# Cached keys turned beside the even layer and kept turned in a scratch area

## The chip, the cores and the metric

The kernel runs on one core of a Trainium2 chip. The metric is the device time of one execution in microseconds (us); lower is better. Engines are named as in the profile: PE (TensorE, the matrix engine), PEld (its weight loads), DVE (VectorE), ACT (ScalarE), POOL (GpSimd) and SP (SyncE, whose queue issues nearly all DMAs).

## The reference

One inference step of a two-layer decoder, for a prompt of 2048 tokens and for 8 sequences of 4 new tokens each ("the sample", 32 tokens), model width 1024. Layer 0 (even) has HGRN2 heads (a gated linear recurrence) beside four heads of forgetting attention; layer 1 (odd) is a gated linear attention (GLA). The part that matters here is the sample's attention over a paged cache: each of 8 sequences owns 16 pages of 128 tokens, 4 heads, 128 values a head, in float32.

```python
k_past = k_pages[page_table].reshape(db, -1, H, dh)
v_past = v_pages[page_table].reshape(db, -1, H, dh)
...
logit_past = jnp.einsum('bthd,bshd->bhts', q, k_past).astype(jnp.float32) * scale \
    + cum_new[..., None] + suffix_past[:, :, None, :]
...
p = jax.nn.softmax(jnp.concatenate([logit_past, logit_new], axis=-1), axis=-1).astype(v.dtype)
return jnp.einsum('bhts,bshd->bthd', p[..., :P], v_past) + jnp.einsum('bhts,bshd->bthd', p[..., P:], v)
```

That is 8 x 16 = 128 pages of keys and as many of values, 256 KB each.

## The kernel before

The kernel has three phases.

**Even layer** (`phase_even`). The prompt is worked in two halves of 1024 tokens (the sample goes with the first). Each half has 16 projection units (`order`), a unit being 256 or so columns of the input weights times all tokens of the half; `staged` (L1261) runs a unit's matmuls and puts, between their steps, the fetch, measuring, scaling and splitting of the weights of the units two and three ahead. In the first half the weights come as float32 into tiles of tag `wr` (three buffers), are split into two float16 parts (tag `w`) and stored to the scratch `wd`; in the second half they are loaded from `wd`, and `wr` isn't used. The recurrences (`lin`) run between units. `staged` also calls `beside(x)` twice a unit, at its second and fourth step, with x = 2j and 2j + 1 for the unit j of 32. For x from 33 on, `beside` fetches and measures the weights of the 20 units of the later projections: `later_unit` (L386) loads them into four tiles of tag `lr` (eight buffers) and takes four reductions (L303) of them.

**Attention** (`phase_fox`). `fox_prompt` runs 16 groups (4 heads by 4 query blocks of 512); a group loads q, k, bias, v and gate (L1375 to L1390) on SP's queue, forms scores (PE L626 to L628), adds bias and takes the maximum (DVE, L1413), exponentiates, turns the weights by PE (L1449), splits them (ACT L1456, DVE L1457) and multiplies them with the values. `fox_sample` is interleaved with it by costs: `until` takes from the one or the other by the sum of the costs that each yields. It first works through the cached keys, then through the cached values:

- Keys: 32 tiles, each of one page of four sequences. `pages` loads four page numbers into SP's registers (L1533) and issues four DMAs (L1546) into a tile of tag `pg` (six buffers, shared with the pages of values), 32 partitions a page. `turn` transposes the tile by four DVE instructions in blocks of 32 x 32 (L1590) into a tile of tag `kt` (two buffers), so that the head's dimension lies on the partitions. One tile later `strips` issues 16 matmuls, four heads side by side on strips of the array (L1647; the profile has two records for each). The transposes are held behind a few evictions of the prompt (`KAHEAD`), and the requests of pages behind the eighth request before them (`asked[-8]`).
- Values: 34 steps of pages in the same way, 128 partitions a page, used as they land (L1723).

**Odd layer** (`phase_odd`): output projection of layer 0, then layer 1 and the outputs.

The order of instructions on each engine is made when the kernel is built, by a planner that models their times; `issue_after` puts an instruction behind another one in it. Each engine and SP's queue then work strictly in that order. A tile waits until the tile that had its memory before is free, also across the pools of two phases: the attention's tiles on the right side lie where the even layer's weights and activations were.

Of the kernel before, what the change touches and what calls it, by code (L numbers as in the profile page):

```python
# [8 lines left out]
F32 = mybir.dt.float32  # L9
# [10 lines left out]
P = 128  # L20
# [8 lines left out]
NH = 4  # L29
EPS = 1e-6  # L30
WU = 272
# [3 lines left out]
SC_C = 1350.0  # L35
# [4 lines left out]
EWR = 3  # L40
# [7 lines left out]
REST_P = 18000.0  # L48
REST_S = 12200.0
PG = 6  # L50
PAST = 3
VAHEAD = 3
KAHEAD = 6
# [2 lines left out]
WSPLIT = 4  # L56
# [55 lines left out]
def drain(g):  # L112
    for _ in g:
        pass
# [11 lines left out]
class Kern:  # L126
# [6 lines left out]
    def consts(self):  # L133
        nc, i = self.nc, self.i
        cp = self.ctx.enter_context(self.tc.tile_pool(name="const", bufs=1))
        self.cp = cp

        def col(name, ap, n):
            t = cp.tile([P, n], F32, name=name)
            with nc.allow_non_contiguous_dma(reason="small constant vectors"):  # L140
                nc.sync.dma_start(t, ap.rearrange("(k p) -> p k", p=P))
            return t

        self.ident = cp.tile([P, P], F32, name="ident")
# [241 lines left out]
    def later_unit(self, pool, pps, w, cols, key, undo=None):  # L386

        nc = self.nc
        h, width, t = KT // WSPLIT, sum(n for _, n in cols), {}

        def fetch():
            t["raw"] = [pool.tile([P, h, WU], F32, tag="lr", name=f"lr_{key}{a}") for a in range(WSPLIT)]
            for a, off, n, src in self.sources(w, cols, h):
                with nc.allow_non_contiguous_dma(reason="a few columns"):
                    nc.sync.dma_start(t["raw"][a][:, :, off : off + n], src)

        def parts():
            t["m"] = pool.tile([P, WSPLIT + 1], F32, tag="rm", name=f"rm_{key}")
            return [r[:, :, :width] for r in t["raw"]]

        return (fetch,) + self.unit_scale(key, parts, lambda: t["m"], pool, pps, key, undo, 1.0)

# [716 lines left out]
    def phase_even(self):  # L1119
        tc, nc, i = self.tc, self.nc, self.i  # L1120
        def pool(name, **kw):
            return tc.tile_pool(name=name, bufs=1, reuse_waits="tile", **kw)

        with pool("act", side="right") as ap, pool("w", side="right") as w0, pool("wl", side="right") as wp1, \
                pool("wk") as wp0, pool("nrm") as n0, pool("stt") as sp, pool("ps", space=PSUM) as pp0:
            wpool = Pool(w0, {"w": 3, "wr": EWR, "rm": 2, "pow": 2, "lr": 8})
            wp = Pool(wp0, {"c4": 7, "sam": 1, "v4": 3, "sg": 3, "pd": 1, "kt": 2, "y": EY, "xpad": 1, "vs": 3,
                            "ss": 2, "rs_t": 2, "rs_r": 2}, Pool(wp1, {"c2": EC2, "th": ETH}))
            pps = Pool(pp0, {"pj": 3, "gr": 2, "st": 1, "o": 2})
# [26 lines left out]
            for hf in range(2):  # L1156
# [64 lines left out]
                if hf == 0:  # L1221
# [13 lines left out]
                    ahead = [g[0] for g in nxt[:3]]  # L1235
                else:
                    ahead = []
# [264 lines left out]
    def strips(self, makers, sources):  # L1502
# [8 lines left out]
                last = m()  # L1511
        return last

    def fox_sample(self, fs, pps):


        nc, i = self.nc, self.i
        fc = fs
        n_pool = i["cache_fox_k"].shape[1]

        def one(shape, name, dt=F32):
            return fs.tile(shape, dt, tag=name, name=name)

        regs, asked = [None] * 4, []

        def pages(cache, g, j):

            vals = self.tab[:, 4 * g : 4 * g + 4, j]
            with ExitStack() as st:

                if len(asked) >= 8:
                    st.enter_context(self.tc.issue_after(asked[-8].ins))
                _, regs[:] = nc.values_load_multi_w_load_instructions(  # L1533
                    vals, (mybir.EngineType.SP,), min_val=0, max_val=n_pool - 1)
            t = fs.tile([P, 4, 512], F32, tag="pg", name=f"pg{cache}{g}{j}")
            r = []
            for x in range(4):
                src = i[cache][0, bass.ds(regs[x], 1)]
                if cache == "cache_fox_k":
                    dst, src = t[32 * x : 32 * x + 32], src.rearrange("o (k s) h d -> s (o k) (h d)", s=32)  # L1540
                else:
                    dst, src = t[:, x], src.rearrange("o s h d -> (o s) (h d)")
                with ExitStack() as st:
                    if len(asked) < 8:
                        st.enter_context(self.tc.issue_after(first_v.ins))
                    r.append(nc.sync.dma_start(dst, src))  # L1546
# [37 lines left out]
        def turn(t, g, j):  # L1584

            kt = fs.tile([P, NH * 4, P], F32, tag="kt", name=f"kts{g}{j}")
            for x in range(4):
                steps.append(self.last_l)
                with self.tc.issue_after(steps[max(0, len(steps) - KAHEAD)].ins):
                    ins.append(nc.vector.transpose(kt[:, :, 32 * x : 32 * x + 32],  # L1590
                                                   t[:, x].rearrange("p (a e) -> p a e", e=32)))
                yield SC_C
            kts.append(kt)

        env = {}

# [146 lines left out]
        m = self.spread(ys.rearrange("p h b t -> p (h b t)"), pps, "kt", "ys")  # L1743
# [491 lines left out]
```

## Time and profile before

| | |
|---|---|
| median of 3 runs | 2324.5 us (2317.44 to 2325.11) |
| the profiled execution | 2326.98 us |
| its span | 2325.3 us |
| granted clock of PE, mean | 0.981 |
| DMA traffic | 361.93 MB, mean 156 GB/s |

In the profile a row of a stretch gives, for each engine, the busy time and the number of instructions in it; "PEclk" is the clock granted to PE as a share of full speed, "DMA share" the mean share of the core's 16 DMA engines whose packets were under way (it can pass 1). A row of a group gives line, engine, operation, written tile <- read tiles, shapes and count, then busy time and mean ns, then the idle time of the engine before these instructions and what ended most of it. A row of waits reads: engine and line that waited <- what it waited for: us in total, times, the longest.

### The profile page before, as it was taken

To read this page: it belongs to the slowest core of one execution; us is meant where nothing else is said; L and a number is where in the kernel's file an instruction comes from. 1 tells how busy PE (TensorE), PEld (TensorE's weight loads), DVE (VectorE), ACT (ScalarE), POOL (GpSimd) and SP (SyncE) were. 2 spreads that over 40 slices of the span, in tenths; PEclk is the share of its full clock that TensorE was granted. 3 is DMA by queue.
4 is the path that set the end of the run, shared out by engine and by line. 5 is a ranking of instruction groups with operands and counts; after the bars stand their busy time and mean duration, and the time that the engine had idled before them with its cause. 6 is when DMAs were issued, how large, how long until landed. Compare 5 with 4: busy or idle time off the path is not lost.

```text
span 2325.3 us, 58045 instructions
## 1 busy us (share of the span) xinstructions
PE 2211.1 (95%) x23316; PEld 1578.4 (68%) x23316; DVE 1403.4 (60%) x3138; ACT 992.3 (43%) x2200; POOL 727.7 (31%) x788
## 2 busy tenths in 40 slices
PE   7999999999999997788999999999999999999998
PEld 5677677865755874455446888677677666667887
DVE  7756558525644657897668445366665655547554
ACT  6434344211212223355567443555544644545343
POOL 2223424001201223223346245144451432322232
PEclk9999999999999997899999999999999999999999
DMA  7343444755431379999884969424224431115553
GB/s 238 120 126 102 145 133 153 208 146 157 145 120 66 126 185 234 211 225 266 269 268 154 310 200 260 123 75 146 76 92 94 126 92 58 49 56 164 161 196 150
DMA packets 359536, 361.93 MB, mean 156 GB/s; under 512 B 107889, under 2 KB 302770, under 8 KB 355170
## 3 DMA queue, kind: packets, MB, share of 16 engines
q1 hardware_dynamic: 357122, 351.59, 52.3%
q0 software_dynamic: 2144, 6.62, 0.8%
q8 instruction: 183, 3.00, 0.6%
q14 instruction: 87, 0.71, 0.1%
HBM read 244.80 MB, written 96.42 MB: 147 GB/s over the span
## 4 chain that ended last, share of the span: by engine, by line
PE 60%; DMA 8%; DVE 6%; issue 2%; SPq 2%; ACT 2%; POOL 2%; DVEq 0%; POOLq 0%; ACTq 0%
PE pt_o L626 4%; PE pt_o L627 4%; PE pt_o L628 4%; DMA pgcache_fox_k<-in_cache_fox_k 3%; PE pt_Cv L626 2%; PE pt_Cv L628 2%; PE pt_Cv L627 2%; PE pt L1449 1%; PE pv L1723 1%; PE o_C L910 1%; PE gl_C L757 1%; DMA fsg<-sgd 1%; PE pt_Bv L626 1%; PE pt_Bv L628 1%; PE pt_Bk L628 1%
## 5 line engine op out<-in xcount | busy, mean ns | idle before, releaser
L626 PE MATMUL pt_o<-w_o,act 128*128 128x256 f16 x1024 | 279.0, 273 | 1.4 <-ACT sg1C L683 1.2
L627 PE MATMUL pt_o<-w_o,act 128*128 128x256 f16 x1024 | 279.0, 273 | 0.0
L628 PE MATMUL pt_o<-w_o,act 128*128 128x256 f16 x1024 | 278.8, 273 | 0.0
L626 PEld LDWEIGHTS <-act 128*128 128x128 f16 x2304 | 226.0, 98 | 37.9 <-issue 3.5
L627 PEld LDWEIGHTS <-act 128*128 128x128 f16 x2304 | 226.1, 98 | 31.3 <-issue 2.9
L628 PEld LDWEIGHTS <-act 128*128 128x128 f16 x2304 | 226.0, 98 | 29.9 <-issue 2.0
L790 POOL TENSOR_TENSOR kA<-kA,fA 128x512 f32<-128x512 f32 (+1 forms) x56 | 77.1, 1377 | 340.4 <-PE gl_A L757 275.6
L1421 ACT ACTIVATE L<-L,nm,kc 128x512 f32<-128x512 f32 (+3 forms) x160 | 118.2, 741 | 71.7 <-DVE nm L1419 70.5
L628 PE MATMUL pt_Cv<-w_Cv,act 128*128 128x256 f16 (+1 forms) x512 | 141.4, 276 | 0.0
L626 PE MATMUL pt_Cv<-w_Cv,act 128*128 128x256 f16 (+1 forms) x512 | 141.4, 276 | 0.0
L627 PE MATMUL pt_Cv<-w_Cv,act 128*128 128x256 f16 (+1 forms) x512 | 141.4, 276 | 0.0
L1429 POOL TENSOR_SCALAR L<-L,nm 128x512 f32<-128x512 f32 (+3 forms) x160 | 99.8, 638 | 130.7 <-DVE nm L1425 58.9
L1456 ACT ACTIVATE th<-pt 128x512 f16<-128x512 f32 (+3 forms) x159 | 81.9, 528 | 125.6 <-PE pt L1449 124.7
L790 POOL TENSOR_TENSOR kC<-kC,fC 128x512 f32<-128x512 f32 (+1 forms) x56 | 80.5, 1437 | 138.6 <-PE gl_C L757 92.4
L1449 PE MATMUL pt<-ident,L 128*128 128x128 f32 x544 | 93.6, 288 | 12.7 <-DVE tl L1457 11.7
L1590 DVE STREAM_TRANSPOSE kts<-pgcache_fox_k 128x512 f32<-128x512 f32 x128 | 84.4, 693 | 29.9 <-DMA pgcache_fox_k<-in_cache_fox_k 28.4
L1457 DVE TENSOR_TENSOR tl<-pt,th 128x512 f16<-128x512 f32 (+3 forms) x159 | 93.8, 603 | 13.1 <-ACT th L1456 11.9
L1449 PEld LDWEIGHTS pt<-ident,L 128*128 128x128 f32 x544 | 67.8, 147 | 42.3 <-DVE tl L1457 18.7
L626 PE MATMUL s<-k,q 128*128 128x512 f16 (+3 forms) x160 | 58.4, 366 | 31.5 <-DVE mx L1413 31.2
L789 DVE TENSOR_TENSOR qC<-qC,fC 128x512 f32<-128x512 f32 (+1 forms) x56 | 72.9, 1302 | 21.1 <-PE gl_C L757 21.1
L1923 ACT ACTIVATE vC<-pt_Cv,kc 128x512 f32<-128x512 f32 (+1 forms) x40 | 23.9, 599 | 133.1 <-PE pt_Cv L628 133.0
L789 DVE TENSOR_TENSOR qA<-qA,fA 128x512 f32<-128x512 f32 (+1 forms) x56 | 70.0, 1251 | 12.5 <-PE gl_A L757 12.4
(958 smaller groups left out, 6469.5 us busy)
## 6 DMA issues: line engine op xcount, KB each, us to landing
pgcache_fox_k<-in_cache_fox_k SPq DMA_DIRECT2D x128, 256.0 KB, 9.4
pgcache_fox_v<-in_cache_fox_v SPq DMA_DIRECT2D x128, 256.0 KB, 4.5
yr<-yT SPq DMA_DIRECT2D x16, 1024.0 KB, 7.2
x1d<-xo SPq DMA_DIRECT2D x44, 256.0 KB, 4.7
wr_o<-in_w_out_even SPq DMA_DIRECT2D x32, 256.0 KB, 5.3
xo<-in_x_prompt SPq DMA_DIRECT2D x32, 256.0 KB, 5.1
wr_Cv<-in_w_in_odd SPq DMA_DIRECT2D x32, 256.0 KB, 3.6
x1r<-x1d SPq DMA_DIRECT2D x16, 512.0 KB, 4.4
```

The lines of the kernel that those rows point to most:

```text
L626: nc.tensor.matmul(ps, lh[0], rh[0], start=first, stop=False)
L627: nc.tensor.matmul(ps, lh[0], rh[1], start=False, stop=False)
L628: return nc.tensor.matmul(ps, lh[1], rh[0], start=False, stop=last)
L789: nc.vector.tensor_tensor(xv[:, :, 1], xv[:, :, 1], t0.to_broadcast([P, nb, w]), ALU.mult)
L790: nc.gpsimd.tensor_tensor(kv[:, :, 0], kv[:, :, 0], t1.to_broadcast([P, nb, w]), ALU.mult)
L1421: self.last_exp = nc.scalar.activation(lt[:, :w], lt[:, :w], AF.Exp, bias=nm[:, 0:1], scale=ib, accum_out=nm[:, 2 + j : 3 + j])
L1429: nc.gpsimd.tensor_scalar(lt[:, :w], lt[:, :w], nm[:, 1:2], 2.0**14, ALU.mult, ALU.mult)
L1449: nc.tensor.transpose(pt[:, w : w + P], rows[b][s // 4][0][:, (s % 4) * P : (s % 4 + 1) * P], self.ident)
L1456: nc.scalar.activation(th[:, a:w], pt[:, a:w], AF.Copy),
L1457: nc.vector.tensor_tensor(tl[:, a:w], pt[:, a:w], th[:, a:w], ALU.subtract)))
L1590: ins.append(nc.vector.transpose(kt[:, :, 32 * x : 32 * x + 32], t[:, x].rearrange("p (a e) -> p a e", e=32)))
L1923: r = nc.scalar.activation(v[h][:, g : g + cnt], ps[:, :, :256], AF.Copy, scale=c)
```

## The change

Tiles 0 to 27 of the cached keys (`PRE` = 28 of 32) are loaded and transposed in the even layer, stored to a new scratch area `kT` in DRAM, and fetched from it in the attention. The other four go the old way.

- `ahead(pool, y)` is called by each `beside`, with x less 8 (`PRE0`), so from the fifth unit on. At an even step it stores the tile turned in the step before, takes a raw tile, loads the next four page numbers and issues the four page DMAs. At the odd step it takes a second tile and has four DVE transposes turn the raw one into it. Both tiles have tag `lr` while x < 32 (first half) and `wr` from then on. The last store is made after the even layer's last unit.
- `later_unit` takes one tile of four parts instead of four tiles; tag `lr` has two buffers of four times the size.
- In the attention `turned(n)` takes a `pg` tile and fills it by one DMA of 1 MB, 8 KB a partition. It has no register load, is put behind nothing but (for the first two) the prompt's first values load, and is read by the strip matmuls where it landed; the tag `kt` isn't used for it. `strips` waits for that DMA instead of for four transposes. The cost yielded for a tile is the same sum in one piece.

```diff
+PRE = 28
+PRE0 = 8
...
+        self.kT = dp.tile([PRE, P, 4 * 512], F32, name="kT")
...
-            t["raw"] = [pool.tile([P, h, WU], F32, tag="lr", name=f"lr_{key}{a}") for a in range(WSPLIT)]
+            t["raw"] = pool.tile([P, WSPLIT, h, WU], F32, tag="lr", name=f"lr_{key}")
...
-                    nc.sync.dma_start(t["raw"][a][:, :, off : off + n], src)
+                    nc.sync.dma_start(t["raw"][:, a, :, off : off + n], src)
...
-            wpool = Pool(w0, {"w": 3, "wr": EWR, "rm": 2, "pow": 2, "lr": 8})
+            wpool = Pool(w0, {"w": 3, "wr": EWR, "rm": 2, "pow": 2, "lr": 2})
...
             def beside(x):
+                self.ahead(wpool, x)
                 x -= 33
...
             drain(last)
+            self.ahead(wpool, 64)
...
+    def turn_block(self, kt, t, x):
+        return self.nc.vector.transpose(kt[:, :, 32 * x : 32 * x + 32], t[:, x].rearrange("p (a e) -> p a e", e=32))
+
+    def ahead(self, pool, y):
+        y -= PRE0
+        if y % 2:
+            if y // 2 < PRE and y > 0:
+                t, tag = self.key
+                self.key = pool.tile([P, NH * 4, P], F32, tag=tag, name=f"kT{y // 2}"), y // 2
+                for x in range(4):
+                    self.turn_block(self.key[0], t, x)
+            return
+        n = y // 2
+        if 0 < n <= PRE:
+            kt, m = self.key
+            self.nc.sync.dma_start(self.kT[m], kt.rearrange("p a s -> p (a s)"))
+        if 0 <= n < PRE:
+            tag = "lr" if y + PRE0 < 32 else "wr"
+            t = pool.tile([P, 4, 512], F32, tag=tag, name=f"kp{n}")
+            with ExitStack() as st:
+                if n:
+                    st.enter_context(self.tc.issue_after(self.last_page.ins))
+                regs = self.page_regs(n % 2, n // 2)
+            for x in range(4):
+                self.last_page = self.page_load(t, "cache_fox_k", regs[x], x)
+            self.key = t, tag
...
+        def turned(n):
+            kt = fs.tile([P, NH * 4, P], F32, tag="pg", name=f"ktd{n}")
+            with ExitStack() as st:
+                if len(asked) < 8:
+                    st.enter_context(self.tc.issue_after(first_v.ins))
+                d = nc.sync.dma_start(kt.rearrange("p a s -> p (a s)"), self.kT[n])
+            asked.extend([d] * 4)
+            kts.append((kt, [d]))
...
-                yield from turn(pages("cache_fox_k", g, j)[0], g, j)
+                if n < PRE:
+                    turned(n)
+                    yield 4 * SC_C
+                else:
+                    yield from turn(pages("cache_fox_k", g, j)[0], g, j)
...
-            kt = kts.pop(0)
+            kt, made = kts.pop(0)
             self.pks.append(self.strips([score(h, g, j, x, kt, sc) for x in range(4) for h in range(NH)],
-                                        ins[4 * n - 4 : 4 * n]))
+                                        made))
```

More of the change, by code (lines that the diff above doesn't have):

```diff
@@ L391, in fetch @@
         def fetch():
-            t["raw"] = [pool.tile([P, h, WU], F32, tag="lr", name=f"lr_{key}{a}") for a in range(WSPLIT)]
+            t["raw"] = pool.tile([P, WSPLIT, h, WU], F32, tag="lr", name=f"lr_{key}")
             for a, off, n, src in self.sources(w, cols, h):
                 with nc.allow_non_contiguous_dma(reason="a few columns"):
-                    nc.sync.dma_start(t["raw"][a][:, :, off : off + n], src)
+                    nc.sync.dma_start(t["raw"][:, a, :, off : off + n], src)
         def parts():
             t["m"] = pool.tile([P, WSPLIT + 1], F32, tag="rm", name=f"rm_{key}")
-            return [r[:, :, :width] for r in t["raw"]]
+            return [t["raw"][:, a, :, :width] for a in range(WSPLIT)]
         return (fetch,) + self.unit_scale(key, parts, lambda: t["m"], pool, pps, key, undo, 1.0)
@@ L1512, in strips, with page_regs, page_load @@
         return last
+    def page_regs(self, g, j):
+        _, regs = self.nc.values_load_multi_w_load_instructions(
+            self.tab[:, 4 * g : 4 * g + 4, j], (mybir.EngineType.SP,), min_val=0,
+            max_val=self.i["cache_fox_k"].shape[1] - 1)
+        return regs
+    def page_load(self, t, cache, reg, x):
+        src = self.i[cache][0, bass.ds(reg, 1)]
+        if cache == "cache_fox_k":
+            return self.nc.sync.dma_start(t[32 * x : 32 * x + 32], src.rearrange("o (k s) h d -> s (o k) (h d)", s=32))
+        return self.nc.sync.dma_start(t[:, x], src.rearrange("o s h d -> (o s) (h d)"))
+    def turn_block(self, kt, t, x):
[23 more added lines that the diff above has]
+            self.key = t, tag
     def fox_sample(self, fs, pps):
@@ L1518, in fox_sample @@
         fc = fs
-        n_pool = i["cache_fox_k"].shape[1]
         def one(shape, name, dt=F32):
             return fs.tile(shape, dt, tag=name, name=name)
-        regs, asked = [None] * 4, []
+        asked = []
         def pages(cache, g, j):
-            vals = self.tab[:, 4 * g : 4 * g + 4, j]
             with ExitStack() as st:
@@ L1532, in pages @@
                     st.enter_context(self.tc.issue_after(asked[-8].ins))
-                _, regs[:] = nc.values_load_multi_w_load_instructions(
-                    vals, (mybir.EngineType.SP,), min_val=0, max_val=n_pool - 1)
+                regs = self.page_regs(g, j)
             t = fs.tile([P, 4, 512], F32, tag="pg", name=f"pg{cache}{g}{j}")
@@ L1537, in pages @@
             for x in range(4):
[L1538 to L1542, printed above, removed]
                 with ExitStack() as st:
@@ L1545, in pages @@
                         st.enter_context(self.tc.issue_after(first_v.ins))
-                    r.append(nc.sync.dma_start(dst, src))
+                    r.append(self.page_load(t, cache, regs[x], x))
                 asked.append(r[-1])
             return t, r
+        def turned(n):
[6 more added lines that the diff above has]
+            kts.append((kt, [d]))
         yield S0
@@ L1589, in turn @@
                 with self.tc.issue_after(steps[max(0, len(steps) - KAHEAD)].ins):
-                    ins.append(nc.vector.transpose(kt[:, :, 32 * x : 32 * x + 32],
-                                                   t[:, x].rearrange("p (a e) -> p a e", e=32)))
+                    ins.append(self.turn_block(kt, t, x))
                 yield SC_C
-            kts.append(kt)
+            kts.append((kt, ins[-4:]))
         env = {}
```

## The prediction

> **What bounds the kernel now.** The page first, for the engine that bounds the span; then stretches of the span, to find the stage with the idle time that the change can reach.
>
> ```profile
> PE 2211.1 (95%) x23316; PEld 1578.4 (68%) x23316; DVE 1403.4 (60%) x3138; ACT 992.3 (43%) x2200; POOL 727.7 (31%) x788
> ```
>
> ```profile
> core 0: us, PE busy (x) PEld busy (x) DVE busy (x) ACT busy (x) POOL busy (x), PEclk, DMA share, GB/s
> 100.00:350.00 250.00, 247.65 (x3054) 176.27 (x3054) 147.30 (x313) 99.22 (x235) 83.22 (x64) 0.99 0.38 118
> 350.00:420.00 70.00, 65.14 (x876) 54.77 (x875) 58.75 (x132) 29.93 (x75) 28.58 (x24) 1.00 0.55 182
> 420.00:856.00 436.00, 434.99 (x4562) 296.27 (x4561) 213.71 (x494) 93.83 (x235) 54.01 (x56) 1.00 0.47 137
> 856.00:910.00 54.00, 34.43 (x247) 18.78 (x245) 36.62 (x120) 18.95 (x49) 21.38 (x48) 0.75 1.06 235
> 910.00:1085.00 175.00, 143.17 (x1616) 88.59 (x1614) 153.98 (x453) 80.67 (x192) 55.26 (x97) 0.92 1.07 228
> 1085.00:1235.00 150.00, 142.53 (x928) 73.54 (x929) 105.31 (x353) 84.38 (x203) 57.88 (x103) 0.98 0.78 255
> ```
>
> TensorE is the bound at 95%, and in the even layer (the first three rows) it idles 2.4, 4.9 and 1.0 us. The attention begins at 856. Up to 1085 it works on the cached keys: there TensorE idles 19.6 + 31.8 = **51.4 us**, more than anywhere else; in the values stage behind it, 7.5 us of 150 (5%). In the key stage the DMA share is above 1 and VectorE is busy 190.6 of 229 us (83%). Which of the two holds TensorE up is read from the groups of instructions of TensorE and VectorE in 856 to 1085 (busy time, mean ns | idle time before them and what ended it):
>
> ```profile
> L626 PE MATMUL s<-k,q 128*128 128x512 f16 (+2 forms) x84 | 31.9, 380 | 29.8 <-DVE mx L1413 29.6
> L1449 PE MATMUL pt<-ident,L 128*128 128x128 f32 x222 | 42.3, 303 | 10.9 <-DVE tl L1457 10.9
> L627 PE MATMUL fo<-tl,v 128*128 128x512 f16 (+1 forms) x64 | 23.6, 369 | 5.1 <-DVE tl L1457 5.1
> L1590 DVE STREAM_TRANSPOSE kts<-pgcache_fox_k 128x512 f32<-128x512 f32 x128 | 84.4, 693 | 29.9 <-DMA pgcache_fox_k<-in_cache_fox_k 28.4 <-PE sc L1647 1.6
> ```
>
> TensorE's idle time ends with VectorE: 29.6 + 10.9 + 5.1 = 45.6 us behind evictions of the prompt's attention (L1413, L1457). VectorE in turn has 84.4 us of transposes between these evictions, and stands 28.4 us in front of a transpose whose page has not landed, with the evictions queued behind it. So both resources, in turn, reach TensorE through VectorE.
>
> ```profile
> DMA to landing us min/median/max: 4.7/9.4/12.8
> ```
>
> ```profile
> pgcache_fox_v<-in_cache_fox_v SPq DMA_DIRECT2D x128, 256.0 KB, 4.5
> ```
>
> The first is a K page's landing, the second a V page's: the same 256 KB, 9.4 against 4.5 us. A K page goes to 32 partitions, four rows of 2 KB each (L1540), a V page to 128, one row each. But the K stage is also the fuller one, so the rows don't separate the two causes.
>
> **What the change removes.** 28 of 32 tiles lose their four transposes: 28 x 4 x 0.693 = **78 us of VectorE**, leaving 190.6 - 78 = 113 of 229 us. They lose 112 page DMAs and 28 register loads on SP's queue, and get 28 issues instead. The 28.4 us of waits for pages go with them, but for the share of four tiles. What is late next? TensorE itself, in the main part: it held 95% in the values stage with VectorE at 70% (105.3 of 150) and a DMA share of 0.78. At that density the key stage's 34.43 + 143.17 = 177.6 us of TensorE work take 177.6 / 0.95 = 187 us instead of 229.
>
> Two things speak for more. First, the start is no dense stretch:
>
> ```profile
> 863.98 7.34 DMA pgcache_fox_k<-in_cache_fox_k
> 871.34 2.06 SPq L1384
> ...
> 874.54 0.90 SPq L1533
> ...
> 895.57 6.35 DMA cb<-cbd
> 901.93 9.84 DMA pgcache_fox_k<-in_cache_fox_k
> ```
>
> This chain of waits runs through SP: page issues, then the next prompt group's loads (L1384), register loads (L1533), the third group's, and a bias load behind pages. Register loads and 112 page issues go, but the turned tiles no longer wait for the eighth request before them, so up to six of 1 MB may be issued ahead of the prompt's second group, where two tiles were. I keep half of the start's idle time beyond 5%, (19.6 - 1.7) / 2 = 9 us: 187 + 9 = 196. Second, DMA. The stage moves:
>
> ```profile
> DMA packets 43650, 52.57 MB, mean 230 GB/s; under 512 B 15824, under 2 KB 22248, under 8 KB 43620
> ```
>
> The turned tiles are 28 x 1.049 = 29.4 MB of it, the rest 23.2 MB. Per unit of share the key stage moved 230 / 1.07 = 215 GB/s, the values stage 255 / 0.78 = 327. With turned tiles (8 KB a partition, 128 partitions) at 327 and the rest at 215 the transfers fill 90 + 108 = 198 us; with all at 327, 161 us. So the queue is nearly full still, and 196 sits between. [...] The granted clock (0.75 and 0.92, against 0.98 in the values stage) should rise as the gaps close, which I count as 1 us. Taken: **195 us, a gain of 34**, with bounds 229 (nothing) and 178 (no idle time, a gain of 51). The value lies by the values stage's row, the nearest: same matmul lines, same SP queue, same ring of buffers.
>
> A new wait: a turned tile's buffer is freed by the strip matmuls on TensorE (L1647) instead of by the transposes, so SP holds the fetch of tile n+6 until tile n is scored, and behind it on SP stand the prompt's next loads (q, k, bias, v, gate). No row shows this wait. Below nothing it can't go, since today's pages wait for a buffer of the same ring too; the nearest row above is the existing wait of a transpose for L1647, 1.6 us once. I take 0 and leave 0 to 6 x 1.6 = 10 us in the range.
>
> **What it adds to the even layer.** One tile beside each unit from the fifth on: a register load, four page issues, one store on SP, four transposes on VectorE, 1.05 MB in and out. 16 units take 436 us of the second half, 27 us each; a transpose comes half a unit, some 13 us, behind its page's request. TensorE idles almost nowhere here, so nothing is gained back; the question is only what it loses.
>
> ```profile
> L303 DVE TENSOR_REDUCE rm_o<-lr_o x32: 669/676/678, 372.2 to 707.9; 128x1 f32<-128x512 f32 x32
> its engine sat idle before it (us, times) until:
> who waited for it (us, times):
> ```
>
> ```profile
> L303 DVE TENSOR_REDUCE rm_Cv<-lr_Cv x16: 669/679/710, 515.6 to 632.1; 128x1 f32<-128x512 f32 x12, 128x1 f32<-128x544 f32 x4
> L303 DVE TENSOR_REDUCE rm_Cqk<-lr_Cqk x16: 670/676/678, 526.2 to 644.7; 128x1 f32<-128x512 f32 x16
> L303 DVE TENSOR_REDUCE rm_Cg<-lr_Cg x16: 668/672/677, 539.9 to 657.0; 128x1 f32<-128x512 f32 x16
> ```
>
> These are the nearest rows: the later layers' weights are measured beside the same units, one unit of 1 MB and four reductions of 676 ns each, 20 of them (80 reductions, 54 us of VectorE). The first group waited for no DMA and nothing waited for it, and TensorE was busy 434.99 of 436. Four transposes of 693 ns and the same MB are the same dose again. VectorE goes from 213.7 to 213.7 + 16 x 2.8 = 258 of 436, and in 100 to 350 from 147.3 to some 175 of 250: room enough. Stores have a price in the page too:
>
> ```profile
> wd<-w_Aqf SPq DMA_DIRECT2D x4, 1024.0 KB, 4.6
> ...
> w_Aqf<-wd SPq DMA_DIRECT2D x4, 1024.0 KB, 4.8
> ```
>
> A tile written as 8 KB a partition lands in 4.6 us, and DMA shares of 0.38 and 0.47 leave room: at 215 GB/s, 2.1 MB each 27 us is 0.36 more. SP's queue is in order, and a store waits there for the transposes; but SP already stands up to 21.3 us in one place beside a full TensorE:
>
> ```profile
> SPq L382 <- PE spr_o L290: 37.8, 4, 21.3
> ...
> SPq L395 <- DVE rm_Cg L303: 24.2, 6, 11.4
> ```
>
> I take 0 for these stretches. At the change of halves VectorE is at 58.75 of 70, and the chain of waits runs over it and a load:
>
> ```profile
> 404.39 1.49 DVE w_Bv L357
> ...
> 406.80 1.20 DVE xhl L525
> 408.01 5.86 DMA ny<-in_x_prompt
> ```
>
> Some three tiles fall here: 3 x 2.8 = 8.4 us more, 67 of 70. Between 0 and 8.4 plus a second 5.86 us for the load, 14, I take **4**, since TensorE had 93% here and other evictions share the burden. At the end, the last tile's store precedes the attention's first buffers in the same memory (a store lands in 4.6 us): **1**. Even layer: **+5**, with bounds 0 and 28 x 2.8 + 6 = 84, if VectorE were on the path throughout; the reductions' row speaks against any but a small part of it. Merging the four `lr` tiles into one costs a fetch that waits for all four reductions instead of one, 3 x 0.68 us on a queue that waits up to 11.4 us for the same tiles already: 0.
>
> **Sum.** The profiled execution took 2326.98 us (span 2325.3 and 1.7 around it), 2.5 above the median 2324.5. 2326.98 - 34 + 5 = 2298; from the median 2295.5. Forecast: **2296**.
>
> **Rivals.** (1) *The key stage stays DMA-bound.* Turned tiles move at no better than 215 GB/s a share (or 6 MB ahead hold up the second group of the prompt), or the V pages asked for earlier fill the gap. Then 52.57 MB still need 229 us, less what VectorE's 78 us give in the stretches where it was full with TensorE below 90%: some 10 us. Time: 2326.98 - 10 + 5 = 2322, no change. For: share 1.07. Against: V pages at 327. Chance 0.12.
>
> (2) *The even layer pays, and the kernel gets slower.* VectorE is in order: a transpose whose page is late holds up the evictions behind it, exactly as in the key stage (28.4 us over 10 waits, 2.8 each). If each of 28 tiles does this at 2.8 us, then 28 x 2.8 = 78 us are at stake; the projections have three PSUM tiles (`pj`), so TensorE runs on for a while: say two thirds reach it, 52 + 5. Time: 2327 - 34 + 57 = 2350. It decides above 34 / 28 = 1.2 us a tile. For: pages land in 9.4 us where the queue is full, the lead is 13 us, and some stretches of the even layer are as full:
>
> ```profile
> 450.00:460.00 10.00, 10.00 (x95) 8.96 (x93) 6.15 (x10) 3.31 (x6) 0.00 (x0) 1.00 1.18 250
> ```
>
>  Against: the reductions, which never waited, and TensorE's 10.00 of 10 in this very row.
>
> [...] Chance 0.20.
>
> (3) *More comes out.* The start closes too and the clock rises: 178 to 182 us, at +3: 2326.98 - 49 + 3 = 2281. Chance 0.12. That the transposes stay in the key stage in spite of the change isn't one of the cases: their tiles lie in pools that close before the attention's open.
>
> **How the numbers follow.** Forecast case, 2283 to 2311: 0.56. The measurement tells about 0.3% (7 us) from no change, so faster means below 2317.5. Faster: 0.56 + 0.12 + 0.02 of rival 1 = 0.70; within: the other 0.10 of it; slower: 0.20. The range is 2276 to 2334: all of the forecast case and of rival 1, most of rival 3 (its lower end, 178 us with an even layer at 0, would be 2276) and the lighter tenth of rival 2; what is left out is most of rival 2, 0.18.
>
> **What would show it.** Right: in the changed profile VectorE's transposes stand between 100 and 856 with no wait on a DMA in front of them; TensorE's idle time there stays below 15 us; the key stage shrinks to about 195 us, with DMA still near 1, and TensorE's wait for L1413 falls from 29.6 to a few us; the values stage stays 150. Wrong: a wait for pages in front of the even layer's transposes; weight loads (`w` from `wd`) landing later than 4.8 us with TensorE idle behind them; turned tiles landing at 9 us or more; SP waiting for the strips with prompt loads behind it.

## The result and the profile after

The change makes the kernel slower: 2350.7 us (median of 4 runs, 2345.8 to 2362.3) against 2322.3 us before on the same chips, a ratio of 1.0135 with a 95% interval of 1.0115 to 1.0155. The forecast was 2296 us.

First, stretches of the span in the changed kernel, cut where its stages end (columns as before the prediction: the stretch, its length, busy time of PE, PEld, DVE, ACT, POOL, then granted clock, DMA share, GB/s):

```profile
0.00:100.00 100.00, 75.01 (x508) 53.58 (x509) 71.62 (x197) 52.25 (x107) 21.41 (x50) 0.91 0.78 221
100.00:240.00 140.00, 124.60 (x1629) 86.19 (x1628) 88.16 (x174) 37.93 (x94) 37.50 (x31) 0.94 0.84 248
240.00:390.00 150.00, 148.12 (x1579) 104.45 (x1577) 82.55 (x188) 66.14 (x152) 48.72 (x37) 0.98 0.39 124
390.00:650.00 260.00, 231.58 (x2292) 158.81 (x2291) 154.80 (x338) 55.79 (x122) 34.99 (x28) 0.94 0.95 269
650.00:933.00 283.00, 281.55 (x3133) 196.23 (x3131) 148.78 (x349) 66.85 (x184) 46.74 (x51) 1.00 0.40 126
933.00:1120.00 187.00, 166.10 (x1891) 103.71 (x1892) 134.81 (x473) 99.78 (x243) 80.26 (x150) 0.97 0.93 293
1120.00:1265.00 145.00, 139.64 (x917) 70.42 (x921) 102.07 (x342) 83.38 (x201) 54.79 (x97) 0.99 0.77 250
```

And the same clock times of the even layer in the kernel before:

```profile
0.00:100.00 100.00, 85.23 (x657) 60.44 (x661) 72.58 (x193) 54.43 (x112) 23.34 (x51) 1.00 0.68 208
100.00:240.00 140.00, 139.53 (x1809) 102.68 (x1809) 84.67 (x177) 53.74 (x137) 47.88 (x37) 1.00 0.35 110
240.00:390.00 150.00, 146.21 (x1868) 104.75 (x1866) 96.28 (x203) 61.52 (x134) 55.74 (x43) 0.98 0.43 136
390.00:650.00 260.00, 256.64 (x2587) 174.64 (x2585) 133.40 (x320) 63.44 (x148) 30.30 (x23) 1.00 0.56 161
650.00:855.00 205.00, 204.40 (x2221) 144.37 (x2219) 105.08 (x238) 44.28 (x126) 31.88 (x40) 1.00 0.37 117
```

From the starts and ends of TensorE's groups (the last matmuls of the even layer, the first and last with pages of values) the stages are:

| us | even layer ends | key stage | values stage | the rest after the attention | span |
|---|---|---|---|---|---|
| before | 855 | 233.9 | 146.8 | 1054.3 | 2325.3 |
| changed | 933 | 186.9 | 145.3 | 1049.8 | 2350.3 |

(Between the values stage and the rest lie 35 us of the prompt's attention, in both kernels.)

The key stage gave 47 us, more than forecast. **The even layer took 78 us more**, where 5 were forecast. And the loss stands in three places: 0 to 100 (TensorE idles 25 us instead of 15), 100 to 240 (15 instead of 0.5) and 390 to 650 (28 instead of 3). From 240 to 390 and from 650 on it idles next to nothing, with or without the change. In these three places the granted clock is 0.91 and 0.94 instead of 1.00, and the same work takes longer: summed over the rows, TensorE is busy 861 us in the even layer instead of 832, and idles 72 us instead of 23. So of the 78 us, 49 are idle time and 29 are slower work. The starts of the units' matmuls in the two traces say it more finely: the changed kernel falls 39 us behind up to 253 us, keeps just that distance until 391, and falls another 39 behind up to 682. The view of the tile `kT` in the changed kernel says what stands in these places:

```profile
L1532 DVE STREAM_TRANSPOSE kT<-kp x112: 664/670/714, 45.7 to 639.3; 128x512 f32<-128x512 f32 x112
...
its engine sat idle before it (us, times) until:
  DMA kp<-in_cache_fox_k: 99.3, 20
```

The first transpose runs at 45.7 us, before the fifth unit, which is the first with a tile in the program (its matmuls, of `Bq`, begin at 146), and the last at 639, some 270 us ahead of the last unit, which begins at 912. The program's place of a tile isn't its place on the engines: nothing held it there, so the planner let the tiles follow each other, 14 us apart in the median, in two groups (requested from 39 to 207 us and from 393 to 624). Where no tile stands, nothing is lost. And VectorE stands 99.3 us in front of transposes whose page has not landed, 20 times. One of these waits, in VectorE's timeline of the changed kernel:

```profile
580.71 0.15 DVE L286 RECIPROCAL kc<-kc 128x1 f32<-128x1 f32 x1
589.90 2.49 DVE L1532 STREAM_TRANSPOSE kT<-kp 128x512 f32<-128x512 f32 x4 [9.04 <-DMA kp<-in_cache_fox_k]
592.32 0.25 DVE L295 TENSOR_REDUCE pow_o<-spr_o 128x1 f32<-128x128 f32 x1
```

and in SP's:

```profile
573.68 5.41 SPq L398 DMA_DIRECT2D lr_Cqk<-in_w_in_odd  x5
579.19 0.41 SPq L1548 DMA_DIRECT2D kT<-kT  x1
579.79 2.98 SPq L1528 DMA_DIRECT2D kp<-in_cache_fox_k  x4
```

The four pages are requested from 579.8 to 582.8, behind other loads on SP's queue, and VectorE comes to the transpose at 580.9: it waits 9.0 us, and the scale of a weight unit (L295), small but needed, stands behind it. The lead was to be 13 us and is 1 here. Over the 28 tiles, VectorE is ready for a tile's transposes 8.0 us behind its first request, in the median, and the last of its four pages has landed 10.0 us behind it: the lead is too short for 22 of the 28.

In the key stage the mechanism of the prediction holds. TensorE's groups there, changed kernel:

```profile
L629 PE MATMUL s<-k,q 128*128 128x512 f16 (+2 forms) x86 | 30.9, 360 | 5.5 <-DVE mx L1418 5.0
L1692 PE MATMUL sc<-ktd,qz 128*32 128x128 f32 x896 | 29.8, 280 | 7.2 <-DMA ktd<-kT 6.3 <-DVE qz L1625 0.4 <-issue 0.4
```

TensorE's wait for the prompt's bias and maximum fell from 29.6 to 5.0 us, and 6.3 us of waits for turned tiles came in.

### The profile page after: what moved, and what is told of

It reads as the page before. It is cut to its first block, busy times and chain, and to the rows that moved or that the text cites. A ratio compares the mean times of both kernels' runs of the same rounds, so it can differ in the third digit from the quotient of the medians.

```text
span 2350.3 us, 58071 instructions
## 1 busy us (share of the span) xinstructions
PE 2221.6 (95%) x23316; PEld 1581.5 (67%) x23316; DVE 1395.6 (59%) x3138; ACT 992.1 (42%) x2200; POOL 731.1 (31%) x788
## 4 chain that ended last, share of the span: by engine, by line
PE 46%; DVE 4%; DMA 2%; ACT 2%; issue 2%; POOL 2%; SPq 1%; POOLq 0%; DVEq 0%; ACTq 0%
PE pt_o L629 4%; PE pt_o L630 4%; PE pt_o L631 4%; PE pt L1454 2%; PE pt_Cv L631 2%; PE pt_Cv L629 2%; PE pt_Cv L630 2%; PE pv L1772 1%; PE o_C L913 1%; PE fo L629 1%; PE gl_C L760 1%; PE fo L630 1%; PE fo L631 1%; PE s L629 1%; PE sc L1692 1%
## 5 line engine op out<-in xcount | busy, mean ns | idle before, releaser
L1532 DVE STREAM_TRANSPOSE kT<-kp 128x512 f32<-128x512 f32 x112 | 70.2, 681 | 105.8 <-DMA kp<-in_cache_fox_k 99.3
L629 PE MATMUL pt_Bv<-w_Bv,act 128*128 128x260 f16 (+1 forms) x256 | 71.5, 279 | 6.1 <-DVE Bvs L1074 2.4
L629 PE MATMUL pt_Bk<-w_Bk,act 128*128 128x256 f16 x256 | 71.0, 277 | 2.8 <-DVE Bvs L1074 2.8
## 6 DMA issues: line engine op xcount, KB each, us to landing
ktd<-kT SPq DMA_DIRECT2D x28, 1024.0 KB, 10.6
```

The lines of the kernel that those rows point to most:

```text
L629: nc.tensor.matmul(ps, lh[0], rh[0], start=first, stop=False)
L1532: return self.nc.vector.transpose(kt[:, :, 32 * x : 32 * x + 32], t[:, x].rearrange("p (a e) -> p a e", e=32))
```

## The experiments

The theories: **A**, an in-order engine waits closely behind a page's request, and what is queued behind it reaches TensorE late; **B**, the 78 us of VectorE's work themselves; **C**, the 59 MB of added traffic; **D**, the merged `lr` tiles. The figures behind each run are those of its profiled execution (span and stages); times are medians where several runs were made, beside 2319 to 2324 us of the kernel before in the same jobs. Runs 1, 2, 4, 5 and 7 to 10 are one execution each; those of the changed kernel lie 16 us apart, so a few microseconds between such runs say nothing.

**1. Transposes without pages.**

```diff
-            for x in range(4):
-                self.last_page = self.page_load(t, "cache_fox_k", regs[x], x)
-            self.key = t, tag
+            if not n:
+                self.key_raw = pool.tile([P, 2, 512], F32, tag="kr", name="kp0")
...
+            self.key = self.key_raw, tag
```

> The 28 x 4 transposes and the 28 stores stay in the even layer, but all of them read one raw tile that is loaded once, so no page is requested there: 27 tiles' page loads (28 MB) are left out, and the keys of the first 28 tiles are not the cache's. Theory A (VectorE stands in front of transposes whose page has not landed, 99.3 us over 20 waits in the changed kernel, and TensorE stands behind VectorE): without pages the waits go, the even layer costs at most 10 us more than before, the key stage keeps its 47 us, the time falls to 2280 to 2300 us. Theory B (the 70 us of VectorE's work itself are on the path): the even layer still costs some 70 us, 2340 to 2360 us. Theory C (59 MB more traffic delays the weights): half of the traffic is left, some 2310 to 2325 us.

2326.7 us; even layer 904 (+49), key stage 190.7. Between A and B, and a miss for both. Its waits for pages are gone (2.7 us once), but nothing holds the transposes back any more: they ran from 23.5 to 462.7 us. Two stretches of this run, and of the kernel before:

```profile
30.00:140.00 110.00, 93.32 (x811) 62.12 (x811) 88.24 (x216) 44.39 (x88) 23.76 (x32) 0.93 0.63 228
...
390.00:570.00 180.00, 160.20 (x1407) 121.68 (x1406) 110.53 (x247) 46.47 (x106) 15.93 (x14) 0.93 0.75 233
```

```profile
30.00:140.00 110.00, 105.99 (x1173) 73.56 (x1174) 82.83 (x204) 48.22 (x103) 33.64 (x39) 1.00 0.44 133
...
390.00:570.00 180.00, 176.67 (x1661) 121.06 (x1659) 89.93 (x210) 42.15 (x93) 16.63 (x13) 1.00 0.60 166
```

TensorE idles 13 and 17 us more in them, at a lower clock. So crowding at the start and at the change of halves costs too, without a wait for a page. The transposes follow each other by 4.8 us in the median here, and the chain of work that ended last runs through them: in 30 to 140 us, 18.6% of it are transposes and 8.3% stores that the next transposes wait for, in 390 to 570 us 15.7% and 7.5%. VectorE's work itself can be on the path, then, where it is crowded enough.

**2. Traffic without transposes.**

```diff
-                self.key = pool.tile([P, NH * 4, P], F32, tag=tag, name=f"kT{y // 2}"), y // 2
-                for x in range(4):
-                    self.turn_block(self.key[0], t, x)
+                self.key = t, y // 2
```

> The 28 tiles are loaded and stored in the even layer as in the change, but not transposed: the 112 transposes are left out, so the keys of the first 28 tiles reach the scores unturned. Theory A (VectorE waiting for pages): VectorE has nothing to wait with, the even layer costs at most 10 us, 2280 to 2300 us. Theory B (VectorE's 70 us): the same, 2280 to 2300 us. Theory C (traffic delays the weights): the 78 us in the even layer stay, 2335 to 2360 us, or more since the tiles follow each other more closely.

2316.5 us; even layer 901 (+46), key stage 181.6. Again between them, at the same two places (the second unit's matmuls to the fifth's, then 390 to 570 us), since the loads too ran ahead, from 37 to 553 us. In 390 to 570 the queue of this run is full:

```profile
DMA packets 41726, 53.50 MB, mean 297 GB/s; under 512 B 20464, under 2 KB 31408, under 8 KB 39088
## 3 DMA queue, kind: packets, MB, share of 16 engines
q1 hardware_dynamic: 41711, 53.30, 104.4%
```

It isn't traffic alone either: a store now comes closely behind its pages on SP's queue, and SP stands 25.8 us in front of stores for pages. The 46 and 49 us of the two halves don't add up to the 78 of the whole, so the whole isn't a sum of two doses.

**3. Tiles held in their place.** A small helper notes the last VectorE instruction and the last SP DMA of the program (so the profile of these kernels gives its line, L143, for many instructions).

```diff
-                for x in range(4):
-                    self.turn_block(self.key[0], t, x)
+                with self.tc.issue_after(self.last_dve.ins):
+                    for x in range(4):
+                        self.turn_block(self.key[0], t, x)
...
-            with ExitStack() as st:
-                if n:
-                    st.enter_context(self.tc.issue_after(self.last_page.ins))
+            with self.tc.issue_after(self.last_sp.ins):
                 regs = self.page_regs(n % 2, n // 2)
```

> The change whole, but each tile's requests are put behind the last DMA issue of SP that stands ahead of them in the program, and each tile's transposes behind the last VectorE instruction that stands ahead of them there; so the planner can't pull a tile ahead of its unit, and a transpose comes half a unit (some 13 us) behind its page's request. Theory A: waits for pages fall from 99 us to under 20 us, the even layer costs 5 to 20 us instead of 78, the time is 2285 to 2300 us, faster than both kernels. Theory B: VectorE's work is the same, so 2340 to 2355 us. Theory C: the same MB, but spread over 750 us instead of two stretches of 200 and 240 us: 2300 to 2330 us.

2316.1 us against 2319.0: ratio 0.9984, interval 0.9971 to 0.9997. Even layer 893 (+38), key stage 190.7. Much better than the change, and less than A expected. Waits for pages fell to 33.8 us in 5 times, and one of these, 23.8 us, is at the change of halves. VectorE's timeline and SP's, this run:

```profile
488.89 0.34 DVE L143 TENSOR_SCALAR Bv<-few_Bv,kc 32x256 f32<-32x256 f32 x1
513.01 2.49 DVE L1546 STREAM_TRANSPOSE kT<-kp 128x512 f32<-128x512 f32 x4 [23.77 <-DMA kp<-in_cache_fox_k]
```

```profile
492.61 4.19 SPq L553 DMA_TRANSPOSE act<-xhl  x2
...
501.43 2.61 SPq L143 DMA_DIRECT2D kp<-in_cache_fox_k  x4
```

SP issues the second half's activations here (4 us for two of those DMAs), and the page's request comes behind them, at 501.4, long after VectorE stands ready for it, at 489.2. Up to the eleventh unit, which begins at 298 us (297 before), this run had lost nothing, with six tiles turned. From there to the fourth unit of the second half (553 instead of 526) it loses 26 of the 38: the later start of the second half, and the units just before it, hold most of them.

**4. Only the requests held.** As before without the first hunk.

> As the one before, but only the requests are put behind their place; the transposes may follow as closely as the planner's model of a load allows. Theory A: the tiles are spread, but the lead over the transpose is short again, so most waits for pages stay: 50 to 100 us of waits, even layer 40 to 80 us, time 2320 to 2350 us. If only the crowding of the tiles counts (Theory C, or VectorE's work in dense stretches), this run is as good as the one before: 2285 to 2305 us.

2360.2 us; even layer 952 (+97), key stage 180.0. A's direction, and worse than expected: the transposes follow their requests closely again (VectorE is ready 2.8 us behind the first request, in the median), so VectorE waits for pages, 22 times:

```profile
  DMA kp<-in_cache_fox_k: 145.7, 22
```

But the tiles weren't spread as expected: they follow each other by 14.8 us and are done at 682 us, ahead of most of their units. The last SP DMA that stands ahead of a request in the program is, but for the first tile, the store of the tile before. Once the transposes run early, so does that store, and an edge to it holds nothing.

**5. The merged raw tile alone** (`PRE = 0`, all 32 tiles the old way).

> Only the merging of the four raw tiles of a later unit into one (tag lr: two buffers of four times the size); no tile is turned ahead, all 32 go the old way. Theory D (the merged tile makes the later weights' loads wait for four reductions and holds SP, and is part of what all runs so far lose around the change of halves, 390 to 570 us): even layer 10 us or more longer than before, 2335 us or more. If the merging is free: 2318 to 2330 us, the even layer ends at 855 as before.

2328.7 us in one run; even layer 856, as before. D is out.

**6. 17 tiles beside quiet units**, held in their place; `ahead` takes a list of units.

```diff
-PRE = 28
-PRE0 = 8
+UNITS = [4, 5, 6, 7, 8, 9, 19, 20, 21, 22, 23, 24, 25, 26, 27, 28, 29]
+PRE = len(UNITS)
```

> As the run with both pinned, but only 17 tiles are turned ahead, beside the units 4 to 9 and 19 to 29: none beside the units around the change of halves (10 to 18), where the run with both pinned lost 25 of its 38 us, and none beside the last two; the other 15 tiles go the old way in the attention. Theory A with the place (what is lost is lost where loads and evictions are already late: the start and the change of halves): the even layer loses at most 8 us; the key stage gains 17/28 of 47, some 28 us; the time is 2295 to 2310 us. If each tile costs the same wherever it stands (38 / 28 = 1.4 us): even layer 23 us, time 2315 to 2322 us, no gain.

2299.8 us against 2323.6: ratio 0.9900, interval 0.9880 to 0.9919. Even layer 866 (+10.5), key stage 201.6. Faster than both kernels. One wait for a page, 1.3 us, is left.

**7. The same, transposes free.**

```diff
-                with self.tc.issue_after(self.last_dve.ins):
-                    for x in range(4):
-                        self.turn_block(self.key[0], t, x)
+                for x in range(4):
+                    self.turn_block(self.key[0], t, x)
```

> The 17 tiles beside the same quiet units as in the run before, requests held in their place, but the transposes free again to follow the requests as closely as the planner likes. Theory A (the short lead makes VectorE wait, wherever it is): 5 us of wait a tile come back, 60 to 100 us in all, and the even layer loses 40 to 60 us instead of 10.5: 2325 to 2350 us. If the place alone matters: 2295 to 2305 us as before.

2341.3 us; even layer 912 (+57), key stage 199.6. The same tiles, and 46 us more than run 6 for the even layer, with 68.5 us of waits for pages:

```profile
  DMA kp<-in_cache_fox_k: 68.5, 14
```

What was changed is one edge, on the transposes, but it changes two things. The lead: VectorE is ready 3.3 us behind a tile's first request in the median, instead of 17.2. And the distance: as in run 4 a request follows the store of the tile before, so the tiles come 14.7 us apart instead of 26.5, and the last is turned at 705 us instead of 813. SP's timeline of run 7:

```profile
575.14 0.34 SPq L143 DMA_DIRECT2D kT<-kT  x1
578.62 2.83 SPq L143 DMA_DIRECT2D kp<-in_cache_fox_k  x4
...
588.86 0.34 SPq L143 DMA_DIRECT2D kT<-kT  x1
...
592.97 2.68 SPq L143 DMA_DIRECT2D kp<-in_cache_fox_k  x4
```

The trace says how much the waits account for. The even layer of run 7, and of run 6:

```profile
0.00:912.00 912.00, 852.34 (x9129) 597.58 (x9130) 519.92 (x1198) 277.82 (x656) 185.78 (x194) 0.97 0.58 173
```

```profile
0.00:866.00 866.00, 834.90 (x9132) 590.13 (x9132) 529.29 (x1198) 277.72 (x656) 188.97 (x194) 0.99 0.61 183
```

TensorE idles 59.7 us in run 7 and 31.1 in run 6, 28.6 more; the other 17 are the same work at a lower clock. Laid over VectorE's timeline, 28.7 us of TensorE's idle time in run 7 lie inside VectorE's waits for pages or in the 5 us behind one, which together are 139 of the 912 us (with 3 us behind a wait, 21.9 us of it). Outside them it idles about as much as run 6 does in all. And the units that lose are quiet ones, those beside which run 6 loses little: 23 us up to the eighth unit (1 in run 6) and 33 from the 21st to the 24th (3 in run 6). So the waits carry the loss of run 7, as far as its trace shows; no run has the short distance with a long lead.

**8. Traffic alone, requests held** (run 3 with the edit of run 2).

> As the run with both pinned (28 tiles, units 4 to 31), but the transposes are left out and the raw tile is stored, so the keys of the first 28 tiles reach the scores unturned. It splits the 38 us that the even layer lost there. If transfers delay the loads and the outputs around the change of halves: 25 us or more stay, time 2300 to 2312 us. If VectorE (its 78 us and the 34 us of waits) does it: 0 to 12 us stay, 2280 to 2295 us.

2334.1 us; even layer 918 (+63), key stage 189.8. Read by the expectation it would be the traffic; SP's waits give another reason:

```profile
SPq L143 <- DMA kp<-in_cache_fox_k: 112.7, 45, 6.9
```

Without transposes the store comes closely behind the pages on SP's queue, and SP stands there for pages as VectorE did, with weight and activation loads behind it. As in run 4 the tiles ran ahead, too, with requests 13 us apart from 143 to 627 us, so this run doesn't split the 38 us of run 3.

**9. Transposes alone, held** (run 1 with the first hunk of run 3; 28 tiles).

> As the run with both pinned, but the transposes read one raw tile that is loaded once: 27 tiles' page loads are left out, so the keys of the first 28 tiles are not the cache's; transposes and stores stand in the same places. If VectorE's work itself costs around the change of halves: 20 us or more of the 38 stay, 2300 to 2312 us. If it was the pages (waits and traffic): 0 to 12 us stay, 2280 to 2295 us.

2283.4 us; even layer 864 (+8.8), key stage 192.5. All 112 transposes and 28 stores beside units 4 to 31, the change of halves among them, cost 9 us when no page is waited for. Beside run 1, with the same transposes and stores but nothing held, this is the cleanest pair of the study: 26 us apart they cost 9 us, 4.8 us apart 49. B is out for tiles that keep their place.

**10. Traffic alone, requests and stores held.**

```diff
-            self.nc.sync.dma_start(self.kT[m], kt.rearrange("p a s -> p (a s)"))
+            with self.tc.issue_after(self.last_sp.ins):
+                self.nc.sync.dma_start(self.kT[m], kt.rearrange("p a s -> p (a s)"))
```

> As the run with pinned traffic (28 tiles beside units 4 to 31, no transposes, so the keys of the first 28 tiles reach the scores unturned), but the store too is put behind its place in the program, a unit behind its load; before, it followed the pages closely, SP stood in front of the stores for 112.7 us and the even layer lost 63 us. Theory A in its wider form (any in-order engine that waits closely behind a page's request holds up what is queued behind it, VectorE and SP alike): SP's waits for pages fall below 20 us and the even layer loses 0 to 20 us, time 2275 to 2300 us. If the transfers themselves delay the others: 40 us or more stay, 2315 us or more.

2311.2 us; even layer 881 (+25), key stage 194.1. From 63 to 25 us by holding the stores, which also spreads the requests (143 to 881 us). It misses the 0 to 20 expected, and SP still waits 31.7 us for pages (33 times) instead of under 20. What the 25 us are isn't shown. The view of waits of this run has

```profile
DVE rm_o L143 <- DMA lr_o<-in_w_out_even: 30.0, 2, 23.0
```

reductions that wait for a later layer's weight, 23 us in one place, the same trap with another load. But run 9, without pages, has such waits too (17.8 us in 2) and loses only 9 us. How much of the 25 is bandwidth alone was not separated.

**11. 19 tiles beside quiet units** (3 to 9 and 18 to 29).

> The run with 17 tiles beside quiet units, with two more: units 3 to 9 and 18 to 29, 19 tiles, both requests and transposes pinned. If each tile gives 1.9 us in the key stage as the 17 did (32.3 us) and the two new places are quiet: 2 to 4 us faster than that run, 2294 to 2299 us. If one of the two places is already that of the start or of the change of halves: 2299 to 2306 us.

2289.1 us against 2320.3: ratio **0.9871**, interval 0.9850 to 0.9892, the best kernel of the study. Even layer 866 (+10.6), key stage 191.9: two tiles more took 9.7 us off the key stage, where 4 were expected. That gain per tile isn't even; why was not followed up.

## Why the prediction was wrong

In the table, the lead is the time from a tile's first page request until VectorE is ready for its transposes, the distance that from one tile to the next, both as medians over the tiles, counted in the traces.

| run | lead, us | distance, us | waits in front of transposes for pages, us | even layer, us more |
|---|---|---|---|---|
| 9, transposes alone, held | no pages | 26.1 | 0 | 9 |
| 6, 17 tiles, held | 17.2 | 26.5 | 1.3 | 10.5 |
| 11, 19 tiles, held | 19.4 | 28.5 | 1.3 | 10.6 |
| 3, 28 tiles, held | 17.4 | 28.1 | 33.8 | 38 |
| 1, transposes alone, free | no pages | 4.8 | 2.7 | 49 |
| 7, 17 tiles, transposes free | 3.3 | 14.7 | 68.5 | 57 |
| the change | 8.0 | 13.7 | 99.3 | 78 |
| 4, requests held | 2.8 | 14.8 | 145.7 | 97 |

Runs 2, 8 and 10 have no transposes; they lost 46, 63 and 25 us.

- **The step that failed** is the one of the even layer: "One tile beside each unit from the fifth on", with "a transpose comes half a unit, some 13 us, behind its page's request", and with them the +5, where 78 were measured. I read the place and the lead from the program. On the engines they are what the planner makes of them, and with no edge between a tile and its unit it pulled all tiles ahead, 14 us apart, with VectorE ready 8 us behind a request whose pages took 10 to land. The row of the reductions, on which I priced the dose at nothing, had its own warning: they begin at 372.2 us, ahead of their units, and `lr_o` was already requested at 19.7 us. They never waited, with loads made so long before. The dose was nearly right for tiles in their place (run 9: 9 us for the work, against 5); the place and the wait were not.
- **Rival 2** was this mechanism, at 2350 us and a chance of 0.20. Its price, 2.8 us in each of 28 tiles, came from the key stage; measured were 20 waits of 5.0 us. Its condition, 1.2 us a tile from which it decides, was met: 78 / 28 = 2.8 us a tile. That its 2350 us are the measured time is luck, for its parts are off: the even layer took 78 us instead of its 57, the key stage gave 47 instead of 34, and another 6 us came off behind the key stage. What it missed is that the tiles would run ahead and crowd, in part at the start and at the change of halves, where TensorE idled before too (15 us in 0 to 100). I priced the change of halves at 4 us for three tiles; in run 3 it and the units ahead of it are most of 38.
- **The key stage** was right: 195 us forecast, 187 measured (180 to 194 in the other runs with 28 tiles), TensorE's wait for L1413 down to 5.0 us. A term that was too small is the clock's: it rose from 0.88 to 0.97, and with it TensorE's busy time fell from 177.6 to 166.1 us, where I had counted 1 us. The DMA queue is nearly full as said (share 0.93), but moves 293 GB/s instead of 230, that is 315 per unit of share instead of 215. Whether that comes of the 128 partitions that a turned tile lands on (a page of keys goes to 32) isn't shown: no run here loads keys to 32 partitions and to 128 at the same load.
- **The new wait**, a tile's buffer freed by the scores, is there, as I had named it among the signs of being wrong. SP's waits in 933 to 1120 us have `SPq L1592 <- PE sc L1692: 20.4, 11, 7.5`, L1592 being the fetch of a turned tile. It cost little: the stage shrank by more than forecast, and TensorE waits 6.3 us for turned tiles. A turned tile lands in a median of 10.6 us, which I had named as a sign of failure; with up to six under way it isn't one.
- **The values stage** and the merged tile went as forecast: 145.3 us, and nothing (run 5).
- **Weight loads** that land late were among my signs of being wrong. They did land later, in a median of 5.9 us instead of 4.8 for `w_Aqf` over four loads; that is small beside VectorE's 99.3 us of waits. SP stands for pages as VectorE does: 112.7 us in 45 waits in run 8, 25.8 us in front of stores in run 2.

Shown are that holding the tiles in their place takes most of the loss away (runs 6 and 7 with pages, 10.5 against 57 us; runs 9 and 1 without, 9 against 49), that VectorE's work isn't it where the tiles keep their place (run 9), that the merged tile isn't it (run 5), and that the place counts (runs 3 and 6). That the waits for pages carry the loss where tiles follow each other by some 14 us is read from the trace of run 7. Not separated by a run are the short lead and the short distance, which come together in each run that loads pages and turns them. Open is also how the rest of 25 to 38 us at the change of halves divides between late requests on SP and the queue's bandwidth.

## What to carry to other kernels

A place in the program is no place on an engine: work that is put "beside" something is put there only if an edge holds it (without one, the last tile was turned some 270 us ahead of its unit), so look in the profile for when such work really runs before its lead is priced. Hold both ends, the request and the instruction that waits for it, with half a stage between them (a lead of 17 to 19 us in runs 6 and 11, where 1.3 us of waits were left), and hold them to something that can't move itself: requests that were held behind the store of the tile before ran ahead with it (run 4: 14.8 us apart, done at 682). An instruction that waited for a page held up what was queued behind it, on VectorE (9.0 us in front of one transpose, with the scale of a weight unit behind it) as on SP's queue (112.7 us in run 8). And choose the stretches: 19 tiles beside units where TensorE was full gave 31 us, 28 tiles held everywhere gave 3.

## What was not expected of the hardware

One issue of the DMA that transposes activations holds SP's queue for 1.6 to 5.1 us in run 3, 2.7 in the median (the row has shortest, median and longest in ns), where a request of a page takes 0.34 in the median (0.32 to 1.99). So a request that stands behind a few of them is late by a good part of a unit (six of them took 17 us of the queue from 476.2 to 496.8, ahead of the request at 501.4; a unit takes some 27 us):

```profile
L553 SPq DMA_TRANSPOSE act<-xhl x8: 1635/2668/5102, 460.0 to 495.1; - x8
```

And TensorE's granted clock fell to 0.91 and 0.94 in stretches in which it still was 75% to 89% busy, so what it lost there is more than its idle time (of the 78 us of the even layer, 29 are slower work). The busy share alone doesn't set the clock: in its first 100 us the kernel before was 85% busy and kept 1.00.
